# Strassen sums of the output projection kept on chip, product banks in strict turn, and the next norm's squares taken one layer later

## The chip, the cores and the metric

One core of one Trainium2 chip runs the whole program. The metric is device time in microseconds (us) from launch to end; the three timed runs of the kernel before gave 2311.68, 2315.86 and 2319.44, median 2315.86. A core has five engines that run side by side, each working through its own list of instructions strictly in order: TensorE (PE; its weight loads are listed as PEld), VectorE (DVE), ScalarE (ACT), GpSimd (POOL) and SyncE (SP), which here issues every DMA. An instruction that waits holds up everything behind it on its engine.

## The reference

A trunk of two layers over 2048 tokens of width 1024, in float32:

```
for l in range(DEPTH):                       # DEPTH = 2
    h = rmsnorm(x, norm_g[l])                # mean of squares over the 1024 columns
    z = h @ w_in[l]                          # split into GLA and MLA inputs
    o_gla = gla_mix(...) * silu(g_gate)      # chunked gated linear attention, 4 heads
    o_mla = block_causal_attention(q, k, v) * silu(m_gate)      # softmax attention, 4 heads
    x = x + concatenate([o_gla, o_mla]) @ w_out[l]              # 1024 x 1024
```

The output is x after both layers.

## The kernel before

Each layer has four stages. Pass 1 walks over the 16 tiles of 128 tokens in pairs (a, b): for each tile PE multiplies the activations with three blocks of `w_in` (`mi`, `qk`, `v`), and the gated linear attention runs between these blocks. Pass 2 makes the gates and the first attention inputs, phase B is the softmax attention, and phase C (`phase_c`) is the output projection with the residual, `x + y @ w_out`.

Every large product is done as three matmuls on split numbers: an operand t becomes a rounded high part (ACT copies it) and a low part t − high (DVE or POOL subtracts), and high·high, high·low and low·high are summed in PSUM.

Phase C uses Strassen's scheme in Winograd's form. `w_out` is cut into four blocks, and seven products replace eight: M1, M5, M6, M7, M3, M2, M4, in that order, for each half p = 0, 1 of the tokens. Each product is 16 blocks of three matmuls (line 1448), k outer and i inner, so 48 matmuls. Its left operand is a combination of blocks of `w_out` (A11, S1, N2, S3, S4, A12, A22); A11 and S1 are made in phase B, the others by the jobs `n2`, `s3`, `s4` and `a22` during the products of p = 0. A job takes a staging tile (`ws`) by DMA, combines, and leaves a high part (ACT, L1216 or L1219) and a low part (POOL, L1217, or DVE, L1220). `s4` first makes A12, then adds both parts of N2 on POOL (L1252) for S4; `s3` subtracts on POOL (L1242). Its right operand is a combination of blocks of y (tiles `yr` of 1 MB and `rc` of 256 KB, both loaded from DRAM); `right` combines them on DVE (L1288) and splits them into a `y` tile (L1272, L1273), one product ahead.

Four PSUM banks form a set; there are two, `ca` and `cb`. M1 and M6 and M7 sum up in one set, M5 and M3 in the other, M2 starts the second set anew and M4 goes on in the first. After each product `evict` adds every bank to a tile `xc` on DVE (L1339). For M1, M5 and M6 that sum is stored to DRAM (`scM`) and loaded again into another `xc` tile for M2, M7 and M3; the finished tiles are stored as the next layer's x (`xd`) or as the output. In the first layer ACT also squares each finished tile (L1354), POOL sums the squares (L1355), and the sum goes to DRAM (`sd`). `norm0` at the end of phase C, and later `norm_q` in pass 1 of the second layer, load 512 tokens' sums, reduce them over the partitions with matmuls against ones (L365), and make the norm factors `rt` for four tiles at once.

PE's order is the program's order. The order on DVE, ACT, POOL and SP is set by a scheduler when the program is built, from its own estimates; jobs such as `n2` and `s4` are attached to a product and a step by the table `at(p, j, k, ...)`. Pools decide reuse: a tile with `bufs=6` has six buffers in turn, and a load into the seventh waits for the first to be read.

Of the kernel before, what the change touches and what calls it, by code (L numbers as in the profile page):

```python
# [52 lines left out]
def trunk(ctx: ExitStack, tc: tile.TileContext, x, xT, xt, positions, w_mi, w_qk, w_v, w_gt, w_mg, pk, w3s,  # L53
# [309 lines left out]
    def norm4(pool, ps, ss, q):  # L363
        for i in range(4):
            T.matmul(ps[:, 2 * i:2 * i + 2], lhsT=ss[:, i * P:(i + 1) * P], rhs=ones, start=True, stop=True)  # L365
        v = pool.tile([P, 4], F32, tag="xv", name="xv")
        V.tensor_scalar(out=v, in0=ps[:, 0:8:2], scalar1=1.0 / D, scalar2=None, op0=ALU.mult)
        norm(pool, v, 4 * q, 4)


    def pass1(l, wp, pp, w1, lat, hT01):
# [222 lines left out]
        def pair(p):  # L594
# [22 lines left out]
            if not more:  # L617

                for which, blks in (("gt", (2, 3)), ("mg", (4, 5))):
                    pc = wi_pieces(l, which, pool_stage(wp, 2)(512))  # L620
# [14 lines left out]
                  merge(tail(a), {0: [go(prep_x, b + 2)], 3: [go(norm_s, b + 1), go(norm_load, b + 2)] if l == 0 else [], 6: [go(prep_h, b + 1, 0)]} if more  # L635
# [5 lines left out]
                        {0: [go(prep_h, b + 1, 1)], 4: [go(norm_s, b + 2)] if l == 0 else [go(norm_q, p // 2 + 1)] if p % 2 else []} if more else {}, wl.get(5, {})))  # L641
# [551 lines left out]
    def phase_c(l, wc, pp, yu):  # L1193
# [141 lines left out]
        def evict(p, j, i, ps):  # L1335
            name = prods[j]
            q, m = place(p, name, i)
            t = ops.pop((p, j, i))
# [4 lines left out]
            if not more:
                dma(out[m * P:(m + 1) * P, q * QD:(q + 1) * QD], t)
                return
            dma(xd[q][:, :, m, :], t.rearrange("p (a c) -> p a c", a=4))
            n = ac.setdefault(q, [0, None])
            n[0] += 1
            if n[0] == 1:
                n[1] = wc.tile([P, QD], F32, tag="ac", name="ac", bufs=1)  # L1350
                A.activation(out=n[1], in_=t, func=AF.Square)
                return
# [3 lines left out]
            if n[0] == KT:  # L1356
                dma(sd[q], n[1])

        def norm0():
            ss = wc.tile([P, QD], F32, tag="xc", name="ss", bufs=7)  # L1360
            dma(ss, sd[0])
            norm4(wc, pp.tile([P, 512], F32, tag="cb", name="co", bufs=4), ss, 0)

        xs = {}
# [19 lines left out]
        for k in range(4):  # L1384
            at(0, 0, k, go(n2, k))
            at(0, 1 + k // 2, k % 2 * 2, go(s3, k))
            at(0, 2 + k // 2, k % 2 * 2 + 1, go(s4, k))
            at(0, 4, k, go(a22, k))
        if more:
            for n, which in enumerate(("mi", "qk")):  # L1390
                pc = []
# [10 lines left out]
                for i in range(8):  # L1402
                    at(1, 2 + 2 * n + i // 4, i % 4, go(piece, i))
            for t in range(2):
                for half in range(2):
                    at(1, 5, 3, go(prep_x, t, half))
                    at(1, 6, 1 + t, go(prep_h, t, half))
            at(1, 6, 0, norm0)
# [144 lines left out]
```

## Time and profile before

| | |
|---|---|
| median of three runs | 2315.86 us |
| profiled execution, its own time | 2314.62 us |
| its span, first to last instruction | 2312.5 us |
| granted TensorE clock, mean | 0.985 |
| phase C of the first layer | 979.75 to 1174.08 us |
| pass 1 of the second layer | from 1173.92 us |
| phase C of the second layer | 2129.27 to 2308.70 us |

The page of the profile gives, for each engine, its busy time and a strip of 40 slices of 57.8 us, each digit the busy share in tenths. The strips of DMA show two places where the 16 DMA engines are nearly full, slices 18 to 20 and 38 to 40: these are the two phases C. Finer views are lists by line, lists of who waited for whom, and the instructions in order of time; a bracket at the end of such a row says how long the engine sat idle before it and which engine, tile and line released it.

### The profile page before, as it was taken

To read this page: it belongs to the slowest core of one execution; us is meant where nothing else is said; L and a number is where in the kernel's file an instruction comes from. 1 tells how busy PE (TensorE), PEld (TensorE's weight loads), DVE (VectorE), ACT (ScalarE), POOL (GpSimd) and SP (SyncE) were. 2 spreads that over 40 slices of the span, in tenths; PEclk is the share of its full clock that TensorE was granted. 3 is DMA by queue.
4 is the path that set the end of the run, shared out by engine and by line. 5 is a ranking of instruction groups with operands and counts; after the bars stand their busy time and mean duration, and the time that the engine had idled before them with its cause. 6 is when DMAs were issued, how large, how long until landed. Compare 5 with 4: busy or idle time off the path is not lost.

```text
span 2312.5 us, 37493 instructions
## 1 busy us (share of the span) xinstructions
PE 2214.1 (96%) x12405; PEld 1906.6 (82%) x12405; DVE 1602.4 (69%) x4615; ACT 1364.9 (59%) x3696; POOL 502.6 (22%) x673
## 2 busy tenths in 40 slices
PE   7899999999999999988899999999999999999889
PEld 6788888888899998866778888888888989988667
DVE  5665557776888888677745555677777888785854
ACT  6655456776777777533434545567777777775311
POOL 0000002333222112256510000044332122122700
PEclk8999999999999999999999999999999999999999
DMA  5410124442411111189821111144433011122876
GB/s 189 141 48 31 42 69 142 132 139 92 130 34 48 39 41 61 55 294 290 254 97 42 41 46 42 63 149 138 124 102 119 28 54 41 33 63 85 293 234 200
DMA packets 193154, 246.75 MB, mean 107 GB/s; under 512 B 15344, under 2 KB 126016, under 8 KB 191936
## 3 DMA queue, kind: packets, MB, share of 16 engines
q1 hardware_dynamic: 192960, 244.35, 32.7%
q8 instruction: 98, 1.61, 0.3%
q14 instruction: 96, 0.79, 0.1%
HBM read 167.75 MB, written 76.55 MB: 106 GB/s over the span
## 4 chain that ended last, share of the span: by engine, by line
PE 76%; DVE 7%; DMA 6%; ACT 4%; issue 3%; POOL 3%; SPq 1%; DVEq 0%; POOLq 0%; ACTq 0%
PE tp L95 8%; PE co L1448 6%; PE o L1061 3%; PE sp L986 3%; PE o L1060 3%; PE sp L989 2%; PE o L1059 2%; PE sp L990 2%; PE sp L987 2%; PE sp L988 2%; PE mg L100 2%; PE mg L98 2%; PE mg L99 2%; PE gt L100 2%; PE gt L99 2%
## 5 line engine op out<-in xcount | busy, mean ns | idle before, releaser
L997 DVE TENSOR_SCALAR_CACHE_REDUCE p<-sp 128x512 f32<-128x512 f32 (+5 forms) x304 | 173.1, 573 | 23.1 <-PE sp L990 18.2
L1004 ACT ACTIVATE p<-p,nm 128x128 f32<-128x128 f32 (+15 forms) x128 | 153.9, 1203 | 39.3 <-DVE nm L1003 34.4
L1039 ACT ACTIVATE ph<-tp 128x512 fp32r<-128x512 f32 x224 | 130.4, 593 | 74.6 <-PE tp L95 60.3
L1040 DVE TENSOR_TENSOR pl<-tp,ph 128x512 fp32r<-128x512 f32 x224 | 151.9, 686 | 30.8 <-ACT ph L1039 29.4
L1059 PE MATMUL o<-ph,v 128*128 128x256 f32 x576 | 167.9, 291 | 3.3 <-DVE yT L1071 2.5
L1061 PE MATMUL o<-pl,v 128*128 128x256 f32 x576 | 169.0, 293 | 2.1 <-DVE pl L1040 1.5
L95 PE MATMUL tp<-cst,p 128*128 128x128 f32 x1088 | 167.1, 275 | 2.1 <-ACT gT L1068 1.4
L185 POOL TENSOR_TENSOR ropeu<-kpe,cos 128x256 f32<-128x256 f32 x8 | 6.8, 848 | 716.8 <-DVE Z L548 716.5
L1060 PE MATMUL o<-ph,v 128*128 128x256 f32 x576 | 161.2, 280 | 0.0
L986 PE MATMUL sp<-kn,q 128*128 128x512 f32 (+3 forms) x320 | 130.1, 407 | 9.0 <-ACT q L921 6.7
L95 PEld LDWEIGHTS tp<-cst,p 128*128 128x128 f32 x1088 | 125.2, 141 | 11.9 <-ACT gT L1068 2.3
L1018 POOL TENSOR_SCALAR gt<-gt,rl 128x128 f32<-128x128 f32 x128 | 80.2, 636 | 184.9 <-DVE rl L1016 116.8
L1059 PEld LDWEIGHTS o<-ph,v 128*128 128x128 f32 x576 | 108.9, 189 | 9.5 <-DVE yT L1071 2.9
L987 PE MATMUL sp<-kn,q 128*128 128x512 f32 (+3 forms) x320 | 116.5, 364 | 0.0
L988 PE MATMUL sp<-kn,q 128*128 128x512 f32 (+3 forms) x320 | 116.3, 370 | 0.0
L903 POOL TENSOR_SCALAR gst<-kpe,rk 128x64 f32<-128x64 f32 x128 | 55.3, 446 | 278.0 <-DVE rk L111 108.9
L989 PE MATMUL sp<-kr,q 128*128 128x512 f32 (+3 forms) x320 | 115.1, 367 | 0.4
L1061 PEld LDWEIGHTS o<-pl,v 128*128 128x128 f32 x576 | 108.9, 189 | 7.2 <-DVE pl L1040 2.5
L990 PE MATMUL sp<-kr,q 128*128 128x512 f32 (+3 forms) x320 | 114.2, 368 | 0.0
L1060 PEld LDWEIGHTS o<-ph,v 128*128 128x128 f32 x576 | 108.8, 189 | 2.3
L98 PE MATMUL vp<-wv_h,hT 128*128 128x512 f32 x256 | 108.8, 425 | 1.8 <-ACT wv_h L265 1.8
L98 PE MATMUL qk<-wqk_h,hT 128*128 128x512 f32 x256 | 109.5, 428 | 0.0
(331 smaller groups left out, 7162.9 us busy)
## 6 DMA issues: line engine op xcount, KB each, us to landing
rc<-yd SPq DMA_DIRECT2D x56, 256.0 KB, 4.5
qd<-qs SPq DMA_DIRECT2D x32, 384.0 KB, 2.9
gst<-qd SPq DMA_DIRECT2D x64, 192.0 KB, 2.5
scM<-xc SPq DMA_DIRECT2D x48, 256.0 KB, 3.2
xc<-scM SPq DMA_DIRECT2D x48, 256.0 KB, 4.3
ws<-in_w_out SPq DMA_DIRECT2D x40, 256.0 KB, 5.1
xn<-in_x SPq DMA_DIRECT2D x16, 512.0 KB, 3.3
od<-osn SPq DMA_DIRECT2D x32, 256.0 KB, 2.1
```

Of the source, the lines that this page charges most:

```text
L95: T.transpose(o, i, ident[:k, :k])
L98: T.matmul(o, lhsT=lh, rhs=rh, start=start, stop=False)
L986: T.matmul(o, lhsT=qn[:, 0, ts_], rhs=kn[:, 0, k0:k1], start=True, stop=False)
L987: T.matmul(o, lhsT=qn[:, 0, ts_], rhs=kn[:, 1, k0:k1], start=False, stop=False)
L988: T.matmul(o, lhsT=qn[:, 1, ts_], rhs=kn[:, 0, k0:k1], start=False, stop=False)
L989: T.matmul(o, lhsT=qrr[:, 0, ts_], rhs=kr[:, c0:c1], start=False, stop=False)
L990: T.matmul(o, lhsT=qrr[:, 1, ts_], rhs=kr[:, c0:c1], start=False, stop=True)
L997: V.tensor_scalar(out=pt[:, c0:c0 + w], in0=sp[:, 0:w], scalar1=0.0, scalar2=-3e38, op0=ALU.add, op1=ALU.max, accum_out=mx[:, m:m + 1])
L1004: A.activation(out=pt[:, 0:n], in_=pt[:, 0:n], func=AF.Exp, bias=nm, accum_out=rl[:, i:i + 1])
L1059: T.matmul(o[:, s], lhsT=vh, rhs=ph[:, j, s], start=(kb == 0), stop=False)
L1060: T.matmul(o[:, s], lhsT=vl, rhs=ph[:, j, s], start=False, stop=False)
L1061: T.matmul(o[:, s], lhsT=vh, rhs=pl[:, j, s], start=False, stop=(last and j == 1))
```

## The change

Lines in this section and in the fences of the new kernel are the new kernel's. Four things change, all in phase C and the norm behind it.

- The sums of M1, M5 and M6 stay in their `xc` tiles (three tags of four buffers, `s1`, `s5`, `s2`) until M2, M7 and M3 add to them; M4 reuses the buffers `s5`. The DRAM tensors `scM` and their 24 stores and 24 loads in each phase C are gone. `ws` falls from 6 buffers to 4, `rc` from 4 to 3.
- The order of products becomes M1, M5, M6, M3, M7, M2, M4, and for p = 1 the two sets of banks swap roles, so that no product follows another on the same banks. For that the jobs `s4` come before `s3`.
- The sums of squares are no longer made in phase C. In pass 1 of the second layer ACT squares each tile of x (128x1024), DVE reduces eight columns to one (TENSOR_REDUCE, 128x128 out), and `norm1` makes the factors tile by tile. For tiles 0 and 1 that happens at the end of phase C.
- The low parts of the next layer's `w_in` blocks `mi` and `qk` are all made on DVE, not half of them on POOL.

```diff
         def norm_s(t):
+            if l > 0:
+                sq = w1.tile([P, D], F32, tag="xn", name="xn", bufs=1)
+                A.activation(out=sq, in_=xs[t], func=AF.Square, scale=1.0 / 32.0)
+                sss[t] = w1.tile([P, P], F32, tag="ss", name="ss", bufs=1)
+                V.tensor_reduce(out=sss[t], in_=sq.rearrange("p (k c) -> p c k", k=KT), axis=AX.X, op=ALU.add)
+                return
...
+        def norm_m(t):
+            norm1(w1, pp.tile([P, 8], F32, tag="tp", name="tp"), sss.pop(t), t)
...
+    def norm1(pool, ps, ss, t):
+        T.matmul(ps[:, 0:2], lhsT=ss, rhs=ones, start=True, stop=True)
+        v = pool.tile([P, 1], F32, tag="xv", name="xv")
+        V.tensor_copy(v, ps[:, 0:1])
+        norm(pool, v, t, 1)
...
-        prods = ["M1", "M5", "M6", "M7", "M3", "M2", "M4"]
+        prods = ["M1", "M5", "M6", "M3", "M7", "M2", "M4"]
...
-            return wc.tile([P, 512], F32, tag="ws", name="ws", bufs=6)
+            return wc.tile([P, 512], F32, tag="ws", name="ws", bufs=4)
...
-            t = rc[p, j, k % 4] = wc.tile([P, 512], F32, tag="rc", name="rc", bufs=4)
+            t = rc[p, j, k % 4] = wc.tile([P, 512], F32, tag="rc", name="rc", bufs=3)
...
+        homes = {"M1": "s1", "M5": "s5", "M6": "s2", "M4": "s5"}
         def opload(p, j, i):
             name = prods[j]
+            if name in adds:
+                return
             q, m = place(p, name, i)
-            t = ops[p, j, i] = wc.tile([P, QD], F32, tag="xc", name="xc", bufs=7)
-            if name in adds:
-                dma(t, sc[adds[name], i])
-            elif l == 0:
+            t = ops[p, name, i] = wc.tile([P, QD], F32, tag=homes[name], name="xc", bufs=4)
+            if l == 0:
...
-            t = ops.pop((p, j, i))
+            t = ops[p, adds.get(name, name), i]
             V.tensor_tensor(out=t, in0=ps, in1=t, op=ALU.add)
-            if (name, i) in sc:
-                dma(sc[name, i], t)
+            if name in adds.values():
                 return
...
-            sq = wc.tile([P, QD], F32, tag="sq", name="sq", bufs=1)
-            A.activation(out=sq, in_=t, func=AF.Square)
-            G.tensor_tensor(out=n[1], in0=n[1], in1=sq, op=ALU.add)
...
-            at(0, 1 + k // 2, k % 2 * 2, go(s3, k))
-            at(0, 2 + k // 2, k % 2 * 2 + 1, go(s4, k))
+            at(0, 1 + k // 2, k % 2 * 2, go(s4, k))
+            at(0, 2 + k // 2, k % 2 * 2 + 1, go(s3, k))
...
-            tag = "cb" if name in ("M5", "M3", "M2") else "ca"
+            tag = ("ca", "cb")[(name in ("M5", "M3", "M2")) ^ p]
```

POOL in phase C of the first layer, p = 0, the kernel before. The four rows L1242 subtract for S3 (ws_12249 is k = 0, ws_12294 k = 1, ws_12343 k = 2, ws_12396 k = 3); L1252 adds a part of N2 for S4; ws_12371 is the staging tile of S4's k = 0.

```order
L1217 TENSOR_TENSOR N2l0_12128<-ws_12153,N2h0_12127 128x512
L1242 TENSOR_TENSOR ws_12249<-ws_12249,ws_12251 128x512
L1217 TENSOR_TENSOR N2l0_12128<-ws_12177,N2h0_12127 128x512
L1242 TENSOR_TENSOR ws_12294<-ws_12294,ws_12296 128x512
L1217 TENSOR_TENSOR N2l0_12128<-ws_12197,N2h0_12127 128x512
L1242 TENSOR_TENSOR ws_12343<-ws_12343,ws_12345 128x512
L1217 TENSOR_TENSOR A12l0_12368<-ws_12371,A12h0_12367 128x512
L1242 TENSOR_TENSOR ws_12396<-ws_12396,ws_12398 128x512
L1252 TENSOR_TENSOR ws_12371<-ws_12371,N2h0_12127 128x512
```

All four subtractions stand ahead of the first addition for S4. The same place in the new kernel, from the first low part of S4 to the last; L1240 is now the subtraction for S3, L1250 the addition for S4, L1215 a low part. S4's staging tiles are ws_12231, ws_12277, ws_12329 and ws_12376 (k = 0 to 3), S3's are the pairs ws_12354 and ws_12356 (k = 0) and ws_12396 and ws_12398 (k = 1).

```order
L1215 TENSOR_TENSOR S4l0_12228<-ws_12231,S4h0_12227 128x512
L1250 TENSOR_TENSOR ws_12277<-ws_12277,N2l0_12112 128x512
L1250 TENSOR_TENSOR ws_12329<-ws_12329,N2l0_12112 128x512
L1215 TENSOR_TENSOR S4l0_12228<-ws_12277,S4h0_12227 128x512
L1240 TENSOR_TENSOR ws_12354<-ws_12354,ws_12356 128x512
L1215 TENSOR_TENSOR S4l0_12228<-ws_12329,S4h0_12227 128x512
L1215 TENSOR_TENSOR A12l0_12230<-ws_12376,A12h0_12229 128x512
L1240 TENSOR_TENSOR ws_12396<-ws_12396,ws_12398 128x512
L1250 TENSOR_TENSOR ws_12376<-ws_12376,N2h0_12111 128x512
L1250 TENSOR_TENSOR ws_12376<-ws_12376,N2l0_12112 128x512
L1215 TENSOR_TENSOR S4l0_12228<-ws_12376,S4h0_12227 128x512
```

S4 now comes first, but two subtractions for S3 stand between its k = 0 to 2 and its k = 3.

SP at the same place in the new kernel: the loads behind the first three staging tiles of S4. rc_12315, 12317, 12319 and 12321 are M3's right operands, rc_12501 to 12505 those of M2.

```order
L59 DMA ws_12329<-in_w_out 128x512
L59 DMA rc_12315<-yd1_99 128x512
L59 DMA rc_12317<-yd1_99 128x512
L59 DMA ws_12354<-in_w_out 128x512
L59 DMA rc_12319<-yd1_99 128x512
L59 DMA rc_12321<-yd1_99 128x512
L59 DMA rc_12501<-yd0_98 128x512
L59 DMA rc_12503<-yd0_98 128x512
L59 DMA rc_12505<-yd0_98 128x512
L59 DMA ws_12356<-in_w_out 128x512
L59 DMA ws_12376<-in_w_out 128x512
L59 DMA ws_12396<-in_w_out 128x512
```

The staging tile of S4's k = 3, ws_12376, stands behind M2's loads and one of S3's.

DVE in pass 1 of the second layer in the new kernel, from the state update of one tile (`Z`) to the first use of the next tile's input product (`lr<-mi`); in the kernel before these two rows are neighbours. `xv` to `rt` is `norm1` of the pair's second tile.

```order
L548 TENSOR_TENSOR Z<-kv,Tt 64x2x128 x2
L365 COPY xv<-tp 128x1
L400 TENSOR_REDUCE ss<-xn 128x128
L113 TENSOR_SCALAR xv<-xv 128x1
L107 TENSOR_TENSOR rq<-ry 128x1
L108 TENSOR_TENSOR rq<-rq,xv 128x1
L109 TENSOR_SCALAR rq<-rq 128x1
L110 TENSOR_TENSOR xs<-ry,rq 128x1
L357 COPY rt<-xs 128x1
L358 TENSOR_SCALAR rt<-xs 128x1
L359 TENSOR_TENSOR rt<-xs 128x1
L415 TENSOR_SCALAR lr<-mi,rt 128x2x16
```

Ten instructions have come in between.

## Rows read from the trace of the kernel before

**Rows 1.** The page, busy time: us, share of the span, instructions.

```profile
PE 2214.1 (96%) x12405; PEld 1906.6 (82%) x12405; DVE 1602.4 (69%) x4615; ACT 1364.9 (59%) x3696; POOL 502.6 (22%) x673
```

**Rows 2.** Stretches: window us, length, busy of PE, PEld, DVE, ACT, POOL; PEclk, DMA, GB/s.

```profile
1000.00:1020.00 20.00, 14.46 (x52) 11.37 (x51) 18.04 (x24) 8.28 (x15) 9.36 (x7) 0.83 0.84 278
...
979.75:1075.26 95.51, 82.42 (x338) 65.54 (x338) 70.04 (x85) 34.63 (x59) 58.56 (x40) 0.95 0.88 297
1075.26:1174.08 98.82, 85.13 (x345) 68.74 (x346) 64.31 (x85) 37.42 (x65) 46.01 (x32) 0.91 0.70 220
2129.27:2229.26 99.99, 82.69 (x338) 65.70 (x338) 68.63 (x86) 29.24 (x49) 42.55 (x28) 0.93 0.82 272
2229.26:2308.70 79.44, 79.34 (x336) 64.66 (x336) 40.29 (x63) 13.91 (x22) 0.00 (x0) 0.96 0.65 212
1195.00:1515.00 320.00, 317.45 (x1750) 269.30 (x1749) 185.42 (x594) 165.23 (x541) 0.00 (x0) 1.00 0.16 53
```

**Rows 3.** PE in order of time: start, length, instruction, idle before.

```profile
990.74 0.62 PE L1448 MATMUL co<-y,S1h 128*128 128x512 f32 x2
1001.62 0.39 PE L1448 MATMUL co<-y,N2h 128*128 128x512 f32 x1
1007.55 0.79 PE L1448 MATMUL co<-y,N2h 128*128 128x512 f32 x1 [5.54 <-DVE y L1273]
...
1020.98 0.61 PE L1448 MATMUL co<-y,S3h 128*128 128x512 f32 x2
...
1051.46 0.70 PE L1448 MATMUL co<-y,A12h 128*128 128x512 f32 x2 [1.74 <-DVE xc L1339]
...
2229.26 1.19 PE L1448 MATMUL co<-y,A_h 128*128 128x512 f32 x2 [6.80 <-DVE xc L1339]
```

**Rows 4.** Who PE waited for, 975 to 1180 us: total, times, longest.

```profile
PE co L1448 <- DVE xc L1339: 14.2, 9, 4.1
PE co L365 <- DMA ss<-sd: 5.9, 1, 5.9
PE co L1448 <- DVE y L1273: 5.5, 1, 5.5
PE co L1448 <- POOL S4l L1217: 1.1, 1, 1.1
```

**Rows 5.** DVE in order of time, M5 of p = 0.

```profile
989.05 0.75 DVE L1233 SCALAR_TENSOR_TENSOR ws<-ws,pk,S1h 128x512 f32<-128x512 f32 x1 [6.27 <-DMA ws<-in_w_out]
...
1003.94 0.68 DVE L1235 TENSOR_TENSOR ws<-ws,S1l 128x512 f32<-128x512 f32 x1
...
1005.74 1.75 DVE L1273 TENSOR_TENSOR y<-yr,y 128x512 fp32r<-128x512 f32 x1
```

**Rows 6.** POOL, then ACT, in order of time, p = 0.

```profile
991.27 1.29 POOL L1217 TENSOR_TENSOR N2l<-ws,N2h 128x512 fp32r<-128x512 f32 x1 [15.73 <-ACT N2h L1216]
...
1045.36 1.71 POOL L1217 TENSOR_TENSOR S4l<-ws,S4h 128x512 fp32r<-128x512 f32 x1
...
1004.65 0.63 ACT L1216 ACTIVATE N2h<-ws 128x512 fp32r<-128x512 f32 x1 [1.56 <-DVE ws L1235]
```

**Rows 7.** DMA issues 1010 to 1040 us, median landing; then tile ws, 978 to 1080 us.

```profile
ws<-in_w_out SPq DMA_DIRECT2D x8, 256.0 KB, 3.9
...
rc<-yd SPq DMA_DIRECT2D x4, 256.0 KB, 4.7
...
DMA to landing us min/median/max: 2.6/4.6/6.5
```

**Rows 8.** A pair of pass 1, second layer, in order of time; then DVE by line.

```profile
1224.77 0.25 DVE L415 TENSOR_SCALAR lr<-mi,rt 128x32 fp32r<-128x32 f32 x1 [3.18 <-PE mi L100]
...
1225.17 0.23 DVE L417 SCALAR_TENSOR_TENSOR lr<-mi,rt,lr 128x16 fp32r<-128x16 f32 x1
...
1227.09 0.27 PE L95 MATMUL tp<-cst,lr 128*96 128x128 f32 x1
...
L708 DVE TENSOR_TENSOR hT<-hf,hT 128x1024 fp32r<-128x1024 f32 x32 | 39.9, 1247 | 0.2
```

More of the change, by code (lines that the diff above doesn't have):

```diff
@@ L84, in trunk @@
     xd = [dp.tile([P, 4, KT, P], F32, name=f"xd{q}") for q in range(NQD)]
-    sd = [dp.tile([P, QD], F32, name=f"sd{q}") for q in range(NQD)]
     gd = [dp.tile([P, 512], F32, name=f"gd{t}") for t in range(NT)]
@@ L360, in norm @@
         V.tensor_tensor(out=rt[:, t:t + n, 2], in0=r, in1=r, op=ALU.mult)
[L363 to L368, printed above, removed]
+    def norm1(pool, ps, ss, t):
[3 more added lines that the diff above has]
+        norm(pool, v, t, 1)
     def pass1(l, wp, pp, w1, lat, hT01):
@@ L600, in pair @@
                   merge(bt[0], tail(a - 1) if p else {}, {0: [go(prep_h, b, 0)], 2: [go(prep_h, b, 1)]} if p else {},
-                        {}))
+                        {4: [go(norm_m, b)]} if l > 0 and p else {}))
             lat_chain(a, mi)
@@ L640, in pair @@
                   merge({3: [go(gla_qT, b)], 6: [go(gla_at, b)]},
[L641 removed]
+                        {0: [go(prep_h, b + 1, 1)], 3: [go(norm_m, b + 1)] * (l > 0), 4: [go(norm_s, b + 2)]} if more else {}, wl.get(5, {})))
             gla_v(b, vp)
@@ L1310, in right @@
             rput(p, j, k, t)
-        sc = {(n, i): dp.tile([P, QD], F32, name=f"sc{n}{i}") for n in ("M1", "M5", "M6") for i in range(4)} \
-            if l == 0 else kept[0]
-        kept[0] = sc
         def place(p, name, i):
@@ L1337, in evict @@
             q, m = place(p, name, i)
-            t = ops.pop((p, j, i))
+            t = ops[p, adds.get(name, name), i]
             V.tensor_tensor(out=t, in0=ps, in1=t, op=ALU.add)
-            if (name, i) in sc:
-                dma(sc[name, i], t)
+            if name in adds.values():
                 return
-            if not more:
+            if more:
+                dma(xd[q][:, :, m, :], t.rearrange("p (a c) -> p a c", a=4))
+            else:
                 dma(out[m * P:(m + 1) * P, q * QD:(q + 1) * QD], t)
[L1345 to L1352, printed above, removed]
-            sq = wc.tile([P, QD], F32, tag="sq", name="sq", bufs=1)
-            A.activation(out=sq, in_=t, func=AF.Square)
-            G.tensor_tensor(out=n[1], in0=n[1], in1=sq, op=ALU.add)
[L1356 to L1364, printed above, removed]
+        xs, sss = {}, {}
         def prep_x(t, half):
@@ L1376, in prep_h @@
             V.tensor_tensor(out=hT01[t][:, 1, ks, :], in0=xv, in1=hT01[t][:, 0, ks, :].bitcast(F32), op=ALU.subtract)
+            A.activation(out=xv, in_=xv, func=AF.Square, scale=1.0 / 32.0)
+            if half == 0:
+                sss[t] = wc.tile([P, 512], F32, tag="rc", name="ss", bufs=3)[:, 0:2 * P].rearrange("p (a c) -> p a c", a=2)
+            V.tensor_reduce(out=sss[t][:, half, :], in_=xv.rearrange("p k c -> p c k"), axis=AX.X, op=ALU.add)
+            if half:
+                V.tensor_tensor(out=sss[t][:, 0, :], in0=sss[t][:, 0, :], in1=sss[t][:, 1, :], op=ALU.add)
         go = lambda f, *a: (lambda: f(*a))
@@ L1394, in begin @@
                     width = COLS[which][1]
-                    pc.extend(wi_pieces(l + 1, which, lambda half, k0: wtile().unsqueeze(1)[:, :, 0:width], 1, G))
+                    pc.extend(wi_pieces(l + 1, which, lambda half, k0: wtile().unsqueeze(1)[:, :, 0:width], 1))
                 def piece(i, pc=pc):
@@ L1403, in phase_c @@
                     at(1, 2 + 2 * n + i // 4, i % 4, go(piece, i))
+            at(1, 5, 3, go(prep_x, 0, 0), go(prep_x, 0, 1))
+            at(1, 6, 0, go(prep_x, 1, 0), go(prep_x, 1, 1))
             for t in range(2):
[L1405 to L1408, printed above, removed]
+                at(1, 6, 1 + t, go(prep_h, t, 0), go(prep_h, t, 1))
+                at(1, 6, 3, lambda t=t: norm1(wc, pp.tile([P, 512], F32, tag="ca", name="co", bufs=4), sss[t][:, 0, :], t))
         seq = [(p, j) for p in range(2) for j in range(7)]
@@ L1466, in phase_c @@
         return hT01
-    kept = [None]
     hT01 = {}
```

15 lines of the change are left out of this document (3 added, 12 removed).

## The prediction

> **What bounds the kernel now.** I read the page first: PE is busy for 96% of the span, DVE for 69%, and no other engine is near its limit [rows 1]. So only time in which PE stands or runs slowly can be won. The stretches come next, since the change lies in phase C and pass 1. In pass 1 of the second layer PE is busy for 317.45 of 320 us at full clock; nothing is to be won there, only lost. The four halves of phase C last 95.51, 98.82, 99.99 and 79.44 us [rows 2]. What they could last is read from PE in order of time: M5 starts at 990.74 and M6 at 1001.62 with no wait between, so a product costs 10.88 us and a half 7 × 10.88 = 76.2 us [rows 3]. The four halves are 19.3, 22.6, 23.8 and 3.2 us above that, 69 us in all, and this is the whole prize.
>
> The list of waits says where it goes in the first layer: 14.2 us for the evictions `xc`, 5.9 for the sum of squares that comes back from DRAM (`ss<-sd`), 5.5 for the right operand of M6, 1.1 for S4 [rows 4]; in the second layer one wait for `xc`, at the first product of p = 1, is 6.80 us [rows 3]. Waits cost twice. M6's stage runs from 1001.62 to 1020.98, 19.36 us; less 10.88 and the wait of 5.54 that leaves 2.9 us [rows 3], and the mean granted clock of that stretch is 0.83, so part of it ran at 1.2 instead of 2.4 GHz [rows 2]. A wait of 1.74 us is followed by two matmuls in 0.70 us, which is full pace [rows 3]. So I charge 3 us of slow clock behind a wait of about 5 us and none behind 2.
>
> **Banks and sums kept.** The waits for `xc` come where a product follows another on the same banks: M7 on M6, M2 on M3, and M1 of p = 1 on M4. With sets in strict turn the eviction has a whole product, 10.88 us, to be done. DVE's rows per product in p = 1 are at most 4 evictions, 8 combinations and 4 splits, 16 × 0.68 = 10.9 us [rows 5], which fits because most products have only 12. They also run undisturbed there: a DVE row that takes 0.68 alone took 1.75 beside POOL [rows 5], and after this change POOL has nothing to do in p = 1. So the `xc` waits go. The 48 transfers of 256 KB per phase C go with them, 12.6 MB of the 50 MB that 297 and 220 GB/s move in the first layer [rows 2]. I give them no time of their own; they shorten the other loads, which is counted below.
>
> **The norm at the end of phase C.** The 5.9 us go, since tiles 0 and 1 are squared from x that was stored in p = 0; two matmul pairs stay, 0.5 us. So p = 1 of the first layer should last 76.2 + 0.5 = 76.7 instead of 98.82, a gain of 22.1; in the second layer 76.2 instead of 79.44, a gain of 3.2.
>
> **p = 0 and what is late next.** Here I expect little, because M3 now stands one product earlier and needs S4 10.88 us sooner, while POOL and the loads make S4 no faster. I follow it in the first layer; the second has the same rows.
>
> - DVE's first row still comes at 989.05, bound by a load. Before M6's first split it had 20 rows in 1005.74 − 989.05 = 16.7 us, 0.84 each [rows 5]; now there are 18, so 1004.1. PE then restarts near 1005 instead of 1007.55, a wait of 3 us, and M6 ends near 1017.
> - N2's last combination is the 17th row, done at 1003.1; ACT and POOL (0.63 and 1.3 to 1.7 each, I take 1.5 [rows 6]) give its low part at 1005.4.
> - M6's fourth load waits with three `rc` buffers for the first to be used, so DVE reaches M3's first split at 1011. That frees the buffer for rc_12321, and a load lands after 3.9 (`ws`) to 4.7 (`rc`) us [rows 7]: 1015.4. Its split is done at 1016.7, which lets SP issue rc_12505 and, behind it, ws_12356 at 1017.1, landing at 1021.
> - POOL waits for that tile in its order: the subtraction ends at 1022.5, S4's third low part at 1024. The split of S3's first part frees the buffer for ws_12398: 1024.1 + 3.9 = 1028. Then one subtraction and two additions to 1032.5, S4's last high part at 1033.1 and low part at 1034.6.
> - PE is ready for that k of M3 near 1025.7, waits 7 us, ends M3 at 1037, plus 3 us of slow clock: 1040. S3 comes in time for M7 and A22 for M4, so 3 × 10.88 more end p = 0 at 1072.7.
>
> That is 92.9 us: a gain of 2.6 against 95.51 and of 7.1 against 99.99. Before, the last low part of S4 came at 1045.36 [rows 6] and cost only 1.1 us [rows 4], because M3 came later.
>
> The Trainium skill has a rule on these landings. Its page "SBUF — State Buffer", section "The DMA setup-cost knee", gives a transfer about 2 us plus its bytes at 436 GB/s, an estimated 2.6 us for 256 KB; the trace's shortest is 2.6 and its median 4.6 [rows 7]. By the rule the emptier queues would bring the first rival below.
>
> **Pass 1 of the second layer.** Added per tile: on ACT a square of 128x1024 and two small rows, on DVE a TENSOR_REDUCE over 1024 elements and nine small rows; PE's matmuls against ones stay 16. No row shows the reduce. The nearest has two inputs, 1024 elements and 1.247 us [rows 8]; I take 1.25. Below it can go to half of that, since one input is read and not two; above I let it go to 2.5, twice the row, since it reads across 512 bytes. DVE is busy 185 of 320 us [rows 2], and 14 tiles × (1.25 + 9 × 0.25), the 0.25 from a small row there [rows 8], add 49, so it stays below PE. The place that could cost time is the one where ten rows come in ahead of `lr<-mi`. DVE was idle for 3.18 us there, and its result, ready at 1225.4, was used by PE at 1227.09, 1.7 us later [rows 8]. The ten rows with ACT's two between take about 4 us, so 4 − 3.18 leaves 0.9 of the 1.7. I charge 1 us for the whole stage; with a reduce of 2.5 that is 2.15 of 1.7, 0.45 us over in each of 7 pairs: 3 us. At half of 1.25 it is 0.
>
> The skill's page "SBUF — State Buffer", section on ports and its note on cachelines, says that each access that crosses to a new 16-byte line pays a penalty. By it every element of this reduce would pay; no run here shows it, and no figure is given. It speaks for the rival on the slow side.
>
> The remaining edit, low parts of `w_in` on DVE instead of POOL, adds 8 rows of about 0.68 [rows 5] in p = 1 of the first layer, hidden beside matmuls as said; without that cover they would cost 5.4 us.
>
> **Sum.** 22.1 + 3.2 + 2.6 + 7.1 − 1 = 34.0 us. The profiled execution took 2314.62 (its span 2312.5 and 2.1 around it), 1.2 below the median of three. 2314.6 − 34 = 2280.6; I say 2280 us.
>
> **Rivals.**
> - *S4 in time.* If every landing in the chain takes 2.6 instead of 4 us and POOL's rows 1.3, rc_12321 lands at 1013.7, ws_12356 at 1018, ws_12398 at 1023.4, and S4 is complete at 1028.6; M3 waits 2.7 us without slow clock and p = 0 ends at 1063.6, 84 us. Then the gains of p = 0 are 11.5 and 16, the sum 52, the time 2263. For it: DMA was busy for 0.88 of p = 0 [rows 2], and a quarter of its bytes goes. Against: the median landing of `ws` was 3.9 even in a quieter stretch.
> - *S4 later still.* Landings of 6.5, the longest [rows 7], put ws_12356 at 1025.8, ws_12398 at 1035.4, S4 at 1042, the end of p = 0 at 1080. p = 0 then loses 4.9 and 0.4 us, the sum is 19, the time 2296. For it: SP's queue is one list, and six fewer buffers make it stand more often.
> - *Slower.* The reduce's strided reads make DVE late in every pair. Up to 1.25 + 0.8 = 2.05 us the slack above takes it; each us beyond falls on PE once in each of 7 pairs. The gain of 35 is gone at 35 / 7 + 2.05 = 7 us, and at 8.5 us, 6.8 times the row, 7 × 6.45 = 45 are lost and the time is 2325. Against it: the chain behind it runs once per tile of 20 us, and DVE has 8 us free in each.
> - *No difference.* Scheduled lists on four engines are new in phase C, and p = 1 may stand for loads behind three `rc` and four `ws` buffers; waits of 27 us in all would leave 2307 to 2315.
>
> **Numbers.** The forecast has 0.58 with its own range 2270 to 2290, S4 in time 0.17, S4 later 0.13, no difference 0.06, slower 0.06. About 0.3%, 7 us, is what a measurement of this kernel can tell from no change. The first three are faster: 0.88. Same: 0.06; slower: 0.06. The range runs from 2256, just below the first rival, to 2302, just above the second, and leaves out the last two and some error of the sums.
>
> **What would show it.** In the profile after: PE's waits for `xc` and for `ss<-sd` gone, `scM` gone from the DMA list; p = 1 of both layers within 2 us of 76.2; a wait for S4 of 5 to 8 us inside M3 of each p = 0, and p = 0 near 93; the reduce near 1.25 us and PE's share in pass 1 as before. I am wrong if PE still waits for evictions in p = 1, if M3 waits for nothing or for over 10 us, or if pass 1 grows by more than 3 us.

## The result, and the profile after

The new kernel takes 2285.04 us (median of four runs, 2284.08 to 2286.77), the old one beside it 2315.02 (2311.68 to 2319.44). The ratio of new to old is 0.987, with a 95% interval of 0.9852 to 0.9889. The prediction was 2280 us, between 2256 and 2302. The profiled execution of the new kernel took 2284.22 us, its span 2282.4.

The page's first line for the new kernel answers to [rows 1]:

```profile
PE 2203.8 (97%) x12405; PEld 1899.4 (83%) x12405; DVE 1624.5 (71%) x4751; ACT 1364.6 (60%) x3706; POOL 444.9 (19%) x629
```

The four halves of phase C and a stretch of pass 1 that begins as long after phase C as that of [rows 2], new kernel, columns as there:

```profile
981.62:1075.40 93.78, 83.11 (x339) 65.91 (x338) 64.58 (x81) 28.80 (x48) 47.44 (x28) 0.93 0.74 234
1075.40:1152.23 76.83, 76.83 (x342) 63.68 (x341) 60.04 (x105) 29.00 (x51) 0.00 (x0) 1.00 0.63 190
2108.21:2202.24 94.03, 82.84 (x339) 65.49 (x338) 64.33 (x81) 28.78 (x48) 47.81 (x28) 0.93 0.69 219
2202.24:2278.56 76.32, 76.32 (x337) 62.88 (x335) 42.32 (x67) 14.55 (x23) 0.00 (x0) 1.00 0.43 142
1173.15:1493.15 320.00, 315.80 (x1739) 267.37 (x1739) 219.04 (x701) 178.41 (x573) 0.00 (x0) 1.00 0.16 50
```

Both halves p = 1 are now full: length and PE's busy time are the same number, at full clock. The halves p = 0 gained less: they last 93.78 and 94.03. So the balance is 22.0 + 3.1 us from p = 1 and 1.7 + 6.0 us from p = 0, less 0.8 us in the stretch from the end of the first phase C to the start of the second (955.98 instead of 955.19) and less 1.9 us because phase C began at 981.62 and not at 979.75, though nothing ahead of it was changed. That is 30.1 us, the difference of the two spans.

Who PE waited for between 975 and 1155 us, new kernel (total, times, longest), against [rows 4]:

```profile
PE co L1432 <- ACT S4h L1214: 5.8, 2, 5.2
PE co L1432 <- POOL S4l L1215: 4.0, 2, 3.6
PE co L1432 <- DVE y L1271: 0.7, 1, 0.7
```

No wait for `xc`, none for `ss<-sd`; what is left is S4. PE in order of time, new kernel, shows where, in the place of [rows 3]:

```profile
1003.49 0.62 PE L1432 MATMUL co<-y,N2h 128*128 128x512 f32 x2
...
1012.73 0.50 PE L1432 MATMUL co<-y,N2h 128*128 128x512 f32 x1 [0.67 <-DVE y L1271]
...
1016.23 0.73 PE L1432 MATMUL co<-y,S4h 128*128 128x512 f32 x2 [0.66 <-ACT S4h L1214]
...
1020.59 0.79 PE L1432 MATMUL co<-y,S4l 128*128 128x512 f32 x1 [3.63 <-POOL S4l L1215]
...
1036.92 1.22 PE L1432 MATMUL co<-y,S4h 128*128 128x512 f32 x2 [5.17 <-ACT S4h L1214]
...
1042.71 0.66 PE L1432 MATMUL co<-y,S3h 128*128 128x512 f32 x2
```

M6 lasts 12.74 us, with the waits of 0.67 and 0.66 in it, and M3 26.48, 15.6 more than 10.88. The waits inside M3 are 9.2 us (3.63 and 5.17 above, and one of 0.41 between them). The other 6.4 us are the slow clock behind them: two matmuls take 1.22 us where 0.62 is full pace, and from 1036.92 to 1042.71 the granted clock is 0.50, which is 1.2 GHz.

Why S4 is late is seen on POOL and DVE (new kernel, in order of time), which answer to [rows 5] and [rows 6]:

```profile
995.76 1.67 POOL L1215 TENSOR_TENSOR N2l<-ws,N2h 128x512 fp32r<-128x512 f32 x1 [1.29 <-ACT N2h L1214]
999.48 7.64 POOL L1215 TENSOR_TENSOR N2l<-ws,N2h 128x512 fp32r<-128x512 f32 x1 [2.05 <-ACT N2h L1214]
1007.08 1.29 POOL L1215 TENSOR_TENSOR A12l<-ws,A12h 128x512 fp32r<-128x512 f32 x1
...
1036.95 1.27 POOL L1215 TENSOR_TENSOR S4l<-ws,S4h 128x512 fp32r<-128x512 f32 x1 [0.74 <-ACT S4h L1214]
```

```profile
999.26 0.68 DVE L1286 TENSOR_TENSOR yr<-rc,yr 128x512 f32<-128x512 f32 x1
999.86 0.68 DVE L1286 TENSOR_TENSOR yr<-yr,rc 128x512 f32<-128x512 f32 x1
...
1005.88 2.47 DVE L1335 TENSOR_TENSOR xc<-co,xc 128x512 f32<-128x512 f32 x4
```

A POOL row of a size that takes 1.3 to 1.8 us in the rest of this half took 7.64. It ended at 1007.12, 1.24 us after DVE began the first row that reads PSUM (1005.88): POOL stood through DVE's whole streak of rows with two inputs in SBUF and ran when the streak ended. DVE in turn ran undisturbed and had M6's operands early. Whether this one row is what made S4 late is tested below.

### The profile page after: what moved, and what is told of

It is laid out like the page before. It is cut to its first block, busy times and chain, and to the rows that moved or that the text cites. A ratio compares the mean times of both kernels' runs of the same rounds, so it can differ in the third digit from the quotient of the medians.

```text
span 2282.4 us, 37344 instructions
## 1 busy us (share of the span) xinstructions
PE 2203.8 (97%) x12405; PEld 1899.4 (83%) x12405; DVE 1624.5 (71%) x4751; ACT 1364.6 (60%) x3706; POOL 444.9 (19%) x629
## 2 busy tenths in 40 slices
DMA packets 178176, 219.46 MB, mean 96 GB/s; under 512 B 13680, under 2 KB 124352, under 8 KB 176960
## 3 DMA queue, kind: packets, MB, share of 16 engines
q8 instruction: 98, 1.61, 0.3%
## 4 chain that ended last, share of the span: by engine, by line
PE 79%; DVE 6%; ACT 5%; DMA 5%; POOL 3%; issue 2%; SPq 1%; DVEq 0%; ACTq 0%; POOLq 0%
PE co L1432 10%; PE tp L94 8%; PE o L1059 3%; PE o L1058 2%; PE mg L99 2%; PE sp L984 2%; PE mg L97 2%; PE mg L98 2%; PE o L1057 2%; PE sp L987 2%; PE gt L99 2%; PE gt L98 2%; PE gt L97 2%; PE sp L985 2%; PE sp L988 2%; PE sp L986 2%
```

## The experiments

Theory: the turn of the banks won p = 1, and p = 0 is held by S4, whose chain on POOL, DVE and the staging tiles is too long for M3's earlier place. Rivals: the relief of the DMA engines won it, or the norm. Times are medians; the old kernel was timed beside each.

### Three parts, taken apart

*The old turn*: the new kernel with the old order of products, sets and jobs.

```diff
-        prods = ["M1", "M5", "M6", "M3", "M7", "M2", "M4"]
+        prods = ["M1", "M5", "M6", "M7", "M3", "M2", "M4"]
...
-            at(0, 1 + k // 2, k % 2 * 2, go(s4, k))
-            at(0, 2 + k // 2, k % 2 * 2 + 1, go(s3, k))
+            at(0, 1 + k // 2, k % 2 * 2, go(s3, k))
+            at(0, 2 + k // 2, k % 2 * 2 + 1, go(s4, k))
...
-            tag = ("ca", "cb")[(name in ("M5", "M3", "M2")) ^ p]
+            tag = "cb" if name in ("M5", "M3", "M2") else "ca"
```

> The changed kernel, with the sums kept on chip and the new norm, but with the old order of products (M1, M5, M6, M7, M3, M2, M4), the old sets of banks and S3's jobs ahead of S4's, so that three pairs of neighbours share a set again (M6 and M7, M3 and M2, M4 and the next M1). Theory (the turn of the banks won most of p = 1): waits for xc come back, about 8 to 14 us over both layers with some slow clock behind the long ones; p = 1 of the first layer 85 to 90 us instead of 76.8, of the second about 79 instead of 76.3; p = 0 about 93 to 96; time 2296 to 2304 us. Rival (fewer transfers and the new norm won it): p = 1 stays below 79 us in both layers, time 2283 to 2289 us.

Measured: 2309.41 us, ratio to the old kernel 0.9967 (0.9955 to 0.9979). PE's waits, first the first layer's phase C, then PE in order of time:

```profile
PE co L1432 <- DVE xc L1335: 14.8, 3, 7.9
```

```profile
1025.19 1.19 PE L1432 MATMUL co<-y,S3h 128*128 128x512 f32 x2 [7.88 <-DVE xc L1335]
...
1084.69 1.19 PE L1432 MATMUL co<-y,A_h 128*128 128x512 f32 x2 [4.25 <-DVE xc L1335]
...
1145.03 1.19 PE L1432 MATMUL co<-y,A12h 128*128 128x512 f32 x2 [2.72 <-DVE xc L1335]
```

The three waits stand at pairs that share a set: M7 behind M6, M1 behind M4, M2 of p = 1 behind M3. p = 1 is 84.55 and 79.80 us, p = 0 100.83 and 100.21. The theory holds but its size was too small: the time lies above the expected range. The turn is worth 24.4 us, of which 11.2 lie in p = 1 and 13.2 in p = 0, where two of the three waits stand. The order of the jobs for S3 and S4 went back with the banks, so its share in p = 0 is not told apart.

*Sums through DRAM*: the new kernel with the 48 transfers back.

```diff
...
             if name in adds.values():
+                dma(sc[name, i], t)
+                dma(t, sc[name, i])
                 return
```

> The changed kernel, but each sum of M1, M5 and M6 is stored to DRAM after its eviction and loaded back into the same tile, so that the 48 transfers of 256 KB per phase C are there again while banks turn strictly. Theory (banks): p = 1 stays at 76 to 78 us in both layers, p = 0 within 3 us of 93.8 and 94.0, time 2283 to 2290 us. Rival (the relief of the DMA engines carried the gain): loads of ws and rc land later, p = 0 is over 97 us and p = 1 over 80 us, time 2294 us or more.

Measured: 2286.39 us, ratio 0.9864 (0.9846 to 0.9882), no different from the new kernel. Halves p = 1:

```profile
1073.48:1150.31 76.83, 76.83 (x342) 63.67 (x341) 58.72 (x103) 29.39 (x51) 0.00 (x0) 1.00 0.85 267
2200.00:2276.33 76.33, 76.32 (x337) 62.88 (x335) 42.14 (x67) 14.55 (x23) 0.00 (x0) 1.00 0.65 217
```

By the page the loads of `ws` land after 5.4 us here, 3.4 in the new and 5.1 in the old kernel, and no half notices (p = 0 is 93.09 and 93.39). The relief of the DMA engines was worth nothing that these runs can tell.

*The norm alone*: the old kernel with the new norm.

```diff
...
-            at(1, 6, 0, norm0)
+                at(1, 6, 3, lambda t=t: norm1(wc, pp.tile([P, 512], F32, tag="cb", name="co", bufs=4), sss[t][:, 0, :], t))
```

> The kernel before with only the norm's part of the change: squares and reduce in pass 1 of the second layer, tiles 0 and 1 at the end of phase C; sums through DRAM, old order, old banks. Theory: the wait ss<-sd of 5.9 us and about 3 us of slow clock behind it go, 0.8 us comes in pass 1: 2306 to 2309 us, p = 1 of the first layer 89 to 91 us instead of 98.8. Rival (the wait only hid others, or the reduce at the end of phase C takes its place): 2312 to 2316 us.

Measured: 2302.24 us, ratio 0.994 (0.9921 to 0.996), 14.4 us faster than the old kernel and more of a gain than expected. p = 1 of the first layer fell from 98.82 to 83.58:

```profile
1076.75:1160.33 83.58, 79.39 (x341) 64.40 (x342) 59.47 (x94) 28.18 (x51) 19.82 (x13) 0.98 0.80 254
```

M4 there shrank from 21.74 to 11.55 us, the wait and the slow clock behind it; and M1 from 16.97 to 12.48, which I had not counted: its four waits for `xc` of 1.0 to 1.7 us are now three of 0.2. POOL's rows in this half fell from 32 [rows 2] to 13, so less stands beside DVE's evictions; that this is the reason is argued, not shown.

From the old kernel beside these runs (2316.65 us) the parts add up in this order: norm −14.4, sums kept on chip with fewer staging tiles (and with them the low parts of `w_in` on DVE and a later load of tile 1) +7.2, turn of the banks −24.4. The +7.2 stands on runs that do not overlap (2300.30 to 2304.91 and 2305.76 to 2312.09), though the two intervals overlap a little. So keeping the sums, with the room that it takes, cost time as long as the banks stood as before; the four things in this step were not taken apart.

### The reduce in pass 1

```diff
                 V.tensor_reduce(out=sss[t], in_=sq.rearrange("p (k c) -> p c k", k=KT), axis=AX.X, op=ALU.add)
+                V.tensor_reduce(out=sss[t], in_=sq.rearrange("p (k c) -> p c k", k=KT), axis=AX.X, op=ALU.add)
```

> The changed kernel with the TENSOR_REDUCE of pass 1 (1.98 us) issued twice per tile, 14 times 1.98 = 27.7 us more on DVE. Theory as in the prediction (behind about 2 us of slack each us of DVE falls on PE once in each of 7 pairs): 7 x 1.9 = 13 us more, 2298 us, with PE waits for lr or tp in pass 1. Rival (the reduce runs where DVE is free): 2284 to 2288 us, no new wait on PE over 2 us in sum.

Measured: 2296.82 us, ratio 0.9917 (0.9893 to 0.994). From phase C to phase C it is 968.77 us, 12.8 more than with one reduce. The price is near the 13 expected, the place is another (PE's longest waits, 1155 to 1500 us):

```profile
PE kv L98 <- DVE vr L536: 4.1, 7, 2.1
PE kv L97 <- ACT vr L535: 2.5, 5, 0.5
PE tp L94 <- DVE qkp L482: 2.1, 1, 2.1
```

The scheduler puts the reduces ahead of `vr`, so PE waits for `vr` and not for `lr`. From phase C to phase C PE stood for 24.7 us instead of 16.8, 7.8 more (6.0 of them in the window above); its busy time grew by the other 5.0 us, at a granted clock of 0.99 instead of 1.00.

### What keeps S4 late

*S3's jobs one product later*, so that nothing of S3 stands in S4's way:

```diff
-            at(0, 1 + k // 2, k % 2 * 2, go(s4, k))
-            at(0, 2 + k // 2, k % 2 * 2 + 1, go(s3, k))
+            at(0, 1, k, go(s4, k))
+            at(0, 3, k, go(s3, k))
```

> The changed kernel with the four jobs s4 attached to M5 and the four jobs s3 to M3, so that no load or row of S3 stands ahead of S4's last part. Theory (S4 was late because S3's rows and loads stood between): S4's last low part comes 7 us earlier or more relative to the start of phase C (it came 55.3 us after it), M3 of p = 0 takes 18 to 21 us instead of 26.5, p = 0 is 86 to 88 us in both layers, time 2269 to 2275 us. Rival 1 (POOL itself is the bound: 20 rows of 1.3 to 1.7 us and a stand of 6 us behind DVE): S4's last part at most 3 us earlier, time 2279 to 2285 us. Rival 2 (S3 becomes late for M7): M7 waits for S3 as long as M3 gained, time 2283 to 2290 us.

Measured: 2285.10 us, ratio 0.9861 (0.9846 to 0.9877), no change. The halves p = 0 are 93.18 and 92.17, 2.5 us less together, but phase C began 3.8 us later. M3 fell to 21.14 us, M7 rose to 16.25:

```profile
1025.49 0.79 PE L1432 MATMUL co<-y,S4l 128*128 128x512 f32 x1 [5.30 <-POOL S4l L1215]
...
1052.19 0.79 PE L1432 MATMUL co<-y,S3h 128*128 128x512 f32 x2 [1.99 <-ACT S3h L1217]
```

The wait went from S4 to S3, the second rival. A stretch of this kernel shows what S4 waited for (POOL's busy time is the fifth figure behind the length):

```profile
1010.30:1038.10 27.80, 19.64 (x74) 14.24 (x72) 21.41 (x20) 9.81 (x17) 27.80 (x19) 0.88 0.38 114
```

POOL is busy for all of 27.80 us: my order of its rows mattered less than their number. S3 behind it was late for another reason as well: POOL stood 2.4, 2.7 and 4.1 us for the loads of S3's staging tiles, between 1038 and 1050. So, first, rows were taken off POOL, each kernel building on the one before.

*A12's low parts on DVE*, then *N2's low parts on DVE too*:

```diff
-            wput("A12", k, t, G)
+            wput("A12", k, t, V)
```

> The kernel with S3's jobs one product later (2285.1 us), and the four low parts of A12 on DVE instead of POOL. Theory (POOL's sum of rows is the bound of p = 0: it stood still for nothing between 10 and 53 us after the start): four rows of 1.3 to 1.7 us go from its chain, S4's last low part comes 46 to 48 us after the start instead of 52.7, S3 follows as much earlier, p = 0 is 86 to 88 us in both layers instead of 93.2 and 92.2, time 2273 to 2277 us. Rival (DVE has no room, its rows for M3's and M2's right operands come late, or S3's loads behind four ws buffers set the pace): p = 0 over 91 us, 2282 us or more.

```diff
-            wput("N2", k, t, G)
+            wput("N2", k, t, V)
```

> As the kernel with A12's low parts on DVE, and the four low parts of N2 on DVE too, so that POOL has nothing to do while DVE runs its streak of rows with two SBUF inputs before M6. Theory (POOL's third row of N2 took 7.64 us because DVE kept it out, and S4 started 6 us late for it): S4's last low part comes 38 to 42 us after the start of phase C, M3 waits less than 2 us, p = 0 is 78 to 83 us, time 2257 to 2268 us; M6 waits 1 to 3 us for y, since DVE has four more rows of 0.6 in front. Rival (POOL's next row is kept out in the same way, or DVE becomes the bound): p = 0 within 2 us of the run with A12 alone.

Measured: 2276.50 us, ratio 0.9835 (0.9815 to 0.9854), and 2280.67, ratio 0.9849 (0.9827 to 0.987); the two are not told apart. The first has the time that was expected, but not by the way: p = 0 was to be 86 to 88 us and is 89.26 and 91.29.

```profile
980.41:1069.67 89.26, 82.48 (x339) 66.16 (x338) 67.80 (x87) 28.22 (x48) 42.45 (x24) 0.94 0.73 243
2101.48:2192.77 91.29, 81.88 (x339) 65.63 (x338) 67.27 (x88) 28.50 (x48) 42.22 (x24) 0.94 0.73 236
```

Against the kernel before it the two halves gain 4.8 us of 8.6; in the profiled execution phase C also began 5.0 us earlier, for a reason that stays open. The second failed: p = 0 is 90.60 and 89.58, as its rival had it. M6 takes 11.56 us instead of 15.29, but POOL's next row is kept out in its turn, until the streak ends, and after S4 it stands for loads:

```profile
1004.68 3.48 POOL L1250 TENSOR_TENSOR ws<-ws,N2h 128x512 f32<-128x512 f32 x1 [28.02 <-DMA rc<-yd]
...
1042.16 1.79 POOL L1240 TENSOR_TENSOR ws<-ws 128x512 f32<-128x512 f32 x1 [6.41 <-DMA ws<-in_w_out]
```

S3's loads wait for the four `ws` buffers. *Room back to the staging tiles*: M1's and M5's sums go through DRAM again, `ws` gets 6 buffers and `rc` 5, with N2's low parts on DVE and on POOL:

```diff
-            t = ops[p, name, i] = wc.tile([P, QD], F32, tag=homes[name], name="xc", bufs=4)
+            t = ops[p, name, i] = wc.tile([P, QD], F32, tag="xc", name="xc", bufs=8)
...
+            if name in adds:
+                dma(t, sc[adds[name], i])
```

> As the kernel with the low parts of A12 and N2 on DVE (2280.7 us), but the sums of M1 and M5 go through DRAM again (32 transfers of 256 KB more per phase C), and the room goes to staging tiles: ws 6 instead of 4, rc 5 instead of 3. Theory (after S4, what is late is S3, whose loads wait for ws buffers that S4 holds: POOL stood 4.0 and 6.4 us for them): M7 takes 11 to 13 us instead of 18.8 and 16.3, p = 0 is 83 to 87 us in both layers, time 2266 to 2273 us. Rival (loads are late because the queue is one list and the DMA engines are busier now): p = 0 stays at 89 to 92 us, time 2278 to 2284 us.

> The same with N2's low parts on POOL as in the changed kernel, only A12's on DVE; beside the run with four ws buffers (2276.5 us) it tells the buffers apart from N2's place. Theory: S3 in time as well, p = 0 is 84 to 88 us, 2267 to 2273 us; M6 still waits 2 to 4 us for y and N2's last part, because POOL's row is kept out by DVE's streak. Rival: 2275 us or more.

Measured: 2271.58 us, ratio 0.981 (0.9789 to 0.9831), and 2269.95, ratio 0.9798 (0.9777 to 0.9819). Both are as expected. M7 is down to 12.03 and 11.24 us in the first layer, p = 0 to 86.31 and 87.62; the second kernel's halves:

```profile
985.77:1073.39 87.62, 80.93 (x338) 64.81 (x338) 67.31 (x87) 28.70 (x48) 46.70 (x24) 0.96 0.86 288
2106.23:2192.53 86.30, 80.26 (x339) 64.29 (x338) 67.92 (x85) 28.50 (x48) 45.81 (x24) 0.96 0.83 281
```

The buffers, paid for with 32 transfers per phase C, are worth 6 to 9 us, in the medians and in the halves p = 0 alike; N2's place makes no difference that can be told.

*A12 made later*, by loads of its own during M7, out of S4's chain and out of DVE's streak:

```diff
-            wput("A12", k, t, V)
...
+        def a12(k):
+            wmake("A12")
+            wput("A12", k, wload(0, 4 + k), G)
...
-            at(0, 4, k, go(a22, k))
+            at(0, 4, k, go(a12, k))
+            at(0, 5, k, go(a22, k))
```

> The kernel with six ws and five rc buffers and N2's low parts on POOL (2270.0 us), but A12 is no longer made inside S4's jobs: it gets four loads of its own during M7, its low parts are back on POOL, and A22 follows during M2. Theory (what is left over 76.2 us in p = 0 is S4's chain on POOL and DVE's streak before M6, and A12's rows stand in both): DVE has 18 instead of 21 rows before M6's second split, M6 takes 12 to 13 us instead of 14.7 and 13.2; S4's chain is 12 rows on POOL after N2's four, M3 takes 14 to 16 us instead of 18.1 and 18.3; p = 0 is 82 to 84 us in both layers instead of 87.6 and 86.3, time 2259 to 2265 us. Rival (POOL stays kept out by the streak as long, and S3 or A12 is late for M7 or M2 instead): p = 0 over 86 us, 2268 us or more.

Measured: 2263.48 us (five runs, 2263.09 to 2269.15), ratio to the old kernel 0.9779 (0.9765 to 0.9793), the fastest of all. Halves p = 0:

```profile
981.58:1066.79 85.21, 78.68 (x338) 62.52 (x338) 67.37 (x83) 28.62 (x48) 49.58 (x28) 1.00 0.88 300
2097.03:2181.18 84.15, 78.75 (x338) 62.50 (x338) 65.75 (x84) 28.38 (x48) 48.10 (x28) 1.00 0.89 296
```

M3 takes 14.46 us, as expected. M6 (13.35) and p = 0 (85.21 and 84.15, where 82 to 84 was expected) are a little over, and M7 rose from 11.24 to 13.77, with waits of up to 1.2 us for S3: part of what the rival said. The longest wait in p = 0 is 1.2 us, and the granted clock is 1.00 where it was 0.93. It moves more bytes than the new kernel (238.35 against 219.46 MB) and gains 21.6 us on it. Of the 6.5 us that it is faster than the kernel before it, the halves p = 0 give 4.6.

POOL's long row is still there:

```profile
999.57 7.64 POOL L1215 TENSOR_TENSOR N2l<-ws,N2h 128x512 fp32r<-128x512 f32 x1 [2.05 <-ACT N2h L1214]
```

So that row alone is not what kept S4 late: with fewer rows behind it and more buffers, hardly a wait is left.

### Why POOL's row took 7.64 us

Two kernels, each run once, ran DVE and POOL alone. In the first each streak's DVE rows all write one tile, in short:

```
for i in range(16): V.tensor_tensor(out=o, in0=za, in1=zb, op=ALU.add)
G.tensor_tensor(out=last, in0=pa, in1=start, op=ALU.subtract)
```

> Not the trunk at all: rows of DVE and POOL on tiles of 128x512 float32 alone, the output is filled with zeros. In eight blocks POOL does three additions while DVE runs a streak of 16 rows of one kind: none, two SBUF inputs, one PSUM and one SBUF input, copy, SCALAR_TENSOR_TENSOR with two SBUF inputs, PSUM and SBUF in turn, again two, none. Then three reduces of 128x1024 to 128x128 across 512 bytes, three over neighbours, three plain additions. Theory (a streak of DVE rows with two SBUF inputs keeps POOL out): POOL's first row takes 1.3 us alone and beside PSUM or copy rows, and as long as the rest of the streak, 7 to 10 us, beside rows with two SBUF inputs. Rival (the two share evenly): POOL's row takes 1.7 to 2.6 us in every block, DVE's rows grow too. Reduce: 1.98 us across 512 bytes; if the stride costs, neighbours take 1.1 to 1.3 us, else 1.98 as well.

POOL's first row with no streak, beside two inputs in SBUF, beside a PSUM input; then DVE's three reduces across 512 bytes and over neighbours:

```profile
6.41 1.26 POOL L98 TENSOR_TENSOR noneP<-pa,start 128x512 f32<-128x512 f32 x1 [4.69 <-DVE start L94]
...
11.15 1.64 POOL L98 TENSOR_TENSOR twoP<-pa,start 128x512 f32<-128x512 f32 x1 [0.80 <-DVE start L94]
...
26.07 1.26 POOL L98 TENSOR_TENSOR psumP<-pa,start 128x512 f32<-128x512 f32 x1 [9.94 <-DVE start L94]
```

```profile
96.31 5.42 DVE L105 TENSOR_REDUCE strided<-big 128x128 f32<-128x1024 f32 x3
101.65 3.46 DVE L108 TENSOR_REDUCE unit<-big 128x128 f32<-128x1024 f32 x3
```

The theory failed here: POOL got its turn after one row. In the second kernel POOL's row comes in the middle of the streak, and in one kind of streak the rows write two tiles in turn, in short:

```
V.tensor_tensor(out=zc, in0=zc, in1=zb, op=ALU.subtract)     # odd rows
V.tensor_tensor(out=o, in0=zb, in1=za, op=ALU.subtract)      # even rows
```

> Not the trunk: rows of DVE and POOL alone, the output is filled with zeros. In nine blocks DVE runs a streak of 20 rows with two SBUF inputs and then four evictions from PSUM, and POOL's one row becomes ready in the middle of the streak, after the sixth row: released by DVE itself, by ACT, with a float32r output, with DVE rows in place, with ACT busy, with loads in flight, all of it at once, with tiles far apart, and last without a streak behind it. Theory (a POOL row that comes late into a running streak is kept out until DVE's next row with a PSUM input): POOL's row takes 8 to 10 us in the blocks with a streak and 1.3 in the last. Rival (the two take turns as in the run before, where POOL's row took 1.64 beside the streak): 1.6 to 2 us in every block, and the 7.64 us have another cause; a single block that differs names it.

POOL's row behind one written tile, and behind two in turn; below it DVE's first PSUM rows of that block:

```profile
32.33 1.71 POOL L112 TENSOR_TENSOR actP<-pa,actM 128x512 f32<-128x512 f32 x1 [16.89 <-ACT actM L106]
...
70.90 8.81 POOL L112 TENSOR_TENSOR placeP<-pa,placeM 128x512 f32<-128x512 f32 x1 [15.66 <-ACT placeM L106]
```

```profile
78.50 2.13 DVE L102 TENSOR_TENSOR placeD<-acc,zb 128x512 f32<-128x512 f32 x3
```

8.81 us, ending 1.21 us after the first PSUM row began, in the two blocks with rows in turn; 1.57 to 1.71 us in the six whose rows all write one tile, whatever ACT, the loads or the type do. Without a streak behind it the row takes 1.27. So the lock-out is real and depends on the streak's make. DVE's rows stand differently in time:

```profile
27.39 3.59 DVE L100 TENSOR_TENSOR actD<-za,zb 128x512 f32<-128x512 f32 x5
...
70.68 0.69 DVE L94 TENSOR_TENSOR zc<-zc,zb 128x512 f32<-128x512 f32 x1
71.28 0.68 DVE L96 TENSOR_TENSOR placeD<-zb,za 128x512 f32<-128x512 f32 x1
```

Five rows that write one tile take 3.59 us, so at 0.69 each they start 0.72 to 0.73 us apart, and each begins when the one ahead has ended. Rows in turn start 0.60 us apart at the same length, so each begins before the one ahead has ended. Whether this, the writing in place or the other operation (subtract for add) decides was not separated.

## Why the prediction held, step by step

- *Product and half, 10.88 and 76.2 us*: right; p = 1 came to 76.83 (forecast 76.7) and 76.32 (76.2). Waits for `xc` and `ss<-sd` are gone, as said.
- *Transfers given no time of their own*: right, shown by the sums through DRAM.
- *M6's wait of 3 us*: wrong in size. DVE's 18 rows took 0.66 each, not 0.84 (990.95 to 1002.88). POOL was kept out, and two subtractions for S3 that had stood beside these rows in the old kernel now came later; the shares of the two were not separated. The wait was 0.67 and M6 12.74 us.
- *M3's wait of 7 us and 3 us of slow clock*: too small. They came to 15.6 us, of which 9.2 are waits, near the 10 that I had named as a sign of being wrong. The forecast had one wait, at the last k; there was another of 3.63 us at the first, for S4's first low part behind the long POOL row. I gave POOL 1.3 to 1.7 us a row; one took 7.64, and most between 1013 and 1031 took 1.7. S4's last low part ended 56.6 us after the start of phase C, forecast 54.9.
- These two terms cancel, because M3 can't end before S4's last part is there: what M6 saves, M3 waits longer. M3 ended 61.1 us after the start of phase C, forecast 60.3, and p = 0 came to 93.78 and 94.03, forecast 92.9. The end of the chain was forecast within 2 us although steps of it were off both ways (DVE's rows shorter, POOL's longer); that sum is right by luck as much as by reasoning.
- *The chain of buffers and loads behind S4's k = 3*: a real bound but not the first. With S3 out of the way M3 became 5.3 us shorter and M7 as much longer; POOL's rows had to go, then the `ws` buffers decided.
- *Pass 1, 1 us, reduce 1.25 us*: the cost was 0.8, the reduce 1.98 us by the line below (busy and mean), inside the slack of 2.05 that I had set. The doubled reduce gave 12.8 us where the slack rule gave 13, though not at the place that the rule names. (In the working, a reduce of 2.5 us takes 0.82 + 1.25 = 2.07 of the slack of 1.7, not 2.15: 2.6 us in 7 pairs, not 3.)

```profile
L400 DVE TENSOR_REDUCE ss<-xn 128x128 f32<-128x1024 f32 x14 | 27.7, 1980 | 0.2
```

- *The rule on cachelines* (the Trainium skill, page "SBUF — State Buffer", section "Specifications (TRN2)": each cross to a new 16-byte line pays): the trace agrees in direction. With nothing beside it the reduce takes 5.42 / 3 = 1.8 us across 512 bytes and 3.46 / 3 = 1.15 over neighbours.
- *The rest of the 4.5 us* between 2280.6 and 2285.0: 1.9 us came ahead of phase C, 2.0 in the two p = 0, 0.2 in p = 1, less 0.2 in pass 1 and 0.3 around the span; the median is 0.8 above the profiled run. Among the trunk kernels here phase C began at 979.75 to 985.77 us with the same work ahead; the cause is open, and halves are compared for that reason.
- *Rivals*: "S4 in time" rested on shorter landings. They did shorten, 5.1 to 3.4 us, and S4 was late all the same. "Slower" needed a reduce of 7 us or more.

## What to carry to other kernels

Before a transfer is taken out for its bandwidth, ask whether anyone waits for it: here the buffers that paid for keeping the sums were worth more than the transfers saved. When one product moves forward, count every row of its operand's chain on the slowest engine, and take rows off that engine before reordering them; reordering handed the wait to the next operand. A long wait costs again in slow clock: behind waits of 9.2 us, the longest 5.17, M3 lost 6.4 us more, while the fastest kernel has 6.6 us of waits in the same half, none over 1.2, at a granted clock of 1.00.

## What the runs showed of the hardware that was not expected

A row on POOL can stand through a whole streak of DVE rows with two SBUF inputs: 6.4 of 7.64 us in the trunk, 7.6 of 8.81 us alone, and it starts when DVE reads PSUM. The Trainium skill, page "SBUF — State Buffer", section "Who interferes with whom", has it that such a DVE instruction contends with GpSimd's reads and that the first to issue blocks the other; the rows beside PSUM (1.26) and beside two SBUF inputs (1.64) agree. It speaks of one instruction; in the trunk POOL stood through eleven in a row. Open is why the old kernel and the one with the norm alone show no row of this kind at the same place: in the old one POOL's third row of N2 came 0.2 us into a DVE row, as here, and took 1.61 us.

```profile
1000.18 1.61 POOL L1217 TENSOR_TENSOR N2l<-ws,N2h 128x512 fp32r<-128x512 f32 x1 [2.50 <-ACT N2h L1216]
```

DVE's rows stood 0.60 us apart there too, so that alone does not keep POOL out.
